# Two transformer blocks on one core: each stage's matmul operand is made around the border to it, and the router works on the raw residual

## The chip, the cores and the metric

One Trainium2 chip, of which the kernel uses one core. The time is that of the device for one launch, in microseconds (us); several runs are made and their median counts. A profile is one more execution, recorded by the hardware profiler. In its rows PE is TensorE's matmul stream, PEld its weight loads, DVE VectorE, ACT ScalarE, SPq the sequencer that issues the DMAs, L170 line 170 of the kernel.

## The reference, cut to what matters

256 tokens of width 1024 go through a first block (not touched here but for its last stages' form) and a second block of two layers, and everything is fp32. Layer one is an attention mix and a feed-forward; layer two is an attention with selected keys and a mixture of eight experts, two for each token. Each stage begins with a norm and a modulation by a vector `c`:

```
h = rms_norm(x, norm_mix) * (1 + sc_m) + sh_m
x = x + g_m * (attention(h @ w_in) @ w_out)
h = rms_norm(x, norm_ffn) * (1 + sc_f) + sh_f
x = x + g_f * swiglu(h, gate, up, down)          # layer one, 2816 wide
# layer two instead of it:
logits = h @ router_w + router_b
top_vals, top_idx = top_k(logits, 2); gates = softmax(top_vals)
x = x + g_f * sum_e combine[:, e] * swiglu(h, exp_gate[e], exp_up[e], exp_down[e])
```

## The kernel before, in words

The 256 tokens are two blocks of 128 (`tb` 0 and 1); the residual `h` stays in SBUF, tokens on the partitions. A product of fp32 numbers is made of three fp32r matmuls (`mm3`, L170 to L172): high part by high part, high part of the operand by low part of the weight, low by high. So each weight that a DMA brings in (`raw`) is split by ACT into a high part `wh` (L161) and by DVE into a low part `wl` (L162), and each operand likewise into `xh` and `xl`. There are 6 buffers for `wh`/`wl` and 6 pairs for operands.

`run(i)` calls the stages one after another: 0 to 4 are the first block, 5 its final norm (made together with the norm of stage 6), 6 `even_mix`, 7 `even_ffn`, 8 `odd_mix`, 9 `moe`, 10 the last norm. A border "6 to 7" is the place where stage 6's last product (`psacc`, four accumulators: two token blocks by two halves of 512 columns) is added to the residual and stage 7's first product starts. What lies between:

- `residual` or `gated_residual`: DVE adds each half to `h`.
- `follow`: the norm of the next stage, ACT's squares (L187), DVE's small `rsqrt` steps (L198 to L204), and `xn`, the normed rows (L264, or L279 in `normed_twice`). `normed_twice` writes the first norm times its gain into an extra tile and then rescales `h` with ACT (L280).
- `gate_rows` (L647, L648): the vector that gates the stage's result is spread over the partitions by two fp32 matmuls with a matrix of ones, and copied to SBUF by ACT.
- `to_T_mod`: eight PE transposes of `xn` per token block (L236), gain and shift on ACT and DVE (L253, L255), and the split into `xh` and `xl`. Then the first product starts for that block.

In `moe` the same is done with `xn`, but for the router (L1269): 8 transposes, modulations and 8 small fp32 matmuls with 8 columns per token block, then the two best scores (L1276 to L1279), the places of the tokens in each expert's list (`tri`, L1292), and the gather of each expert's tokens by matmuls with a 0/1 matrix `sel` (L1348, L1354). The program's text gives no fixed order: the tile framework's scheduler orders the instructions of each engine at build time, and every engine then works through its own row strictly in order. `issued_after(ins)` pins what is made inside it behind an instruction, `hold` pins the weight splits.

## Time and profile before

| | |
|---|---|
| median of 3 runs | 1831.12 us (1830.2 to 1831.45) |
| the profiled execution's own time | 1827.23 us |
| its span | 1825.3 us |
| PE busy | 1762.6 us, 97% |
| DVE busy | 1415.3 us, 78% |
| ACT busy | 1085.7 us, 59% |

The span is what the profile covers; the execution's own time is 1.9 us longer, and this execution was 3.9 us shorter than the median of the runs. [...]

### The profile page before, as it was taken

To read this page: it belongs to the slowest core of one execution; us is meant where nothing else is said; L and a number is where in the kernel's file an instruction comes from. 1 tells how busy PE (TensorE), PEld (TensorE's weight loads), DVE (VectorE), ACT (ScalarE), POOL (GpSimd) and SP (SyncE) were. 2 spreads that over 40 slices of the span, in tenths; PEclk is the share of its full clock that TensorE was granted. 3 is DMA by queue.
4 is the path that set the end of the run, shared out by engine and by line. 5 is a ranking of instruction groups with operands and counts; after the bars stand their busy time and mean duration, and the time that the engine had idled before them with its cause. 6 is when DMAs were issued, how large, how long until landed. Compare 5 with 4: busy or idle time off the path is not lost.

```text
span 1825.3 us, 24502 instructions
## 1 busy us (share of the span) xinstructions
PE 1762.6 (97%) x9045; PEld 1522.3 (83%) x9045; DVE 1415.3 (78%) x2505; ACT 1085.7 (59%) x1717; POOL 11.9 (1%) x37
## 2 busy tenths in 40 slices
PE   8999999999999999999989999999998999999996
PEld 6889788888889798888979878898887888888885
DVE  6658877678767797876777765547976999999997
ACT  5443654446445576554566754446485888877774
POOL 0000000000000000000010000000000000000000
PEclk9999999999999999999999999999998999999998
DMA  8768687667767415676755145555324999899993
GB/s 298 253 204 294 225 282 254 231 226 251 257 218 254 157 65 171 218 258 225 254 164 193 48 138 184 174 172 174 132 77 136 358 322 349 316 336 331 336 360 141
DMA packets 181030, 412.40 MB, mean 226 GB/s; under 512 B 8803, under 2 KB 59174, under 8 KB 180774
## 3 DMA queue, kind: packets, MB, share of 16 engines
q1 hardware_dynamic: 178694, 409.12, 64.7%
q10 hardware_dynamic: 2208, 1.63, 0.3%
q8 instruction: 73, 1.20, 0.3%
q14 instruction: 55, 0.45, 0.1%
HBM read 409.67 MB, written 1.05 MB: 225 GB/s over the span
## 4 chain that ended last, share of the span: by engine, by line
PE 83%; DVE 8%; ACT 5%; DMA 3%; issue 1%; SPq 0%; ACTq 0%; DVEq 0%
PE psa L170 17%; PE psa L171 17%; PE psa L172 17%; PE psacc L170 8%; PE psacc L171 8%; PE psacc L172 8%; PE pstr L236 3%; DVE wl L162 2%; ACT wh L161 2%; PE psa L1354 1%; DMA raw<-in_ffn_pre_wd 1%; DMA raw<-in_ffn_pre_wu 1%; ACT sg L789 1%; PE pstr L1385 1%; DVE big L588 1%
## 5 line engine op out<-in xcount | busy, mean ns | idle before, releaser
L162 DVE TENSOR_TENSOR wl<-raw,wh 128x1024 fp32r<-128x1024 f32 (+2 forms) x720 | 816.7, 1157 | 272.6 <-ACT wh L161 266.3
L161 ACT ACTIVATE wh<-raw 128x1024 fp32r<-128x1024 f32 (+2 forms) x720 | 712.1, 1008 | 502.9 <-PE psa L172 271.4
L170 PE MATMUL psa<-wh,xh 128*128 128x512 f32 (+3 forms) x1536 | 569.6, 372 | 16.6 <-ACT xh L161 11.0
L171 PE MATMUL psa<-wl,xh 128*128 128x512 f32 (+3 forms) x1536 | 564.3, 368 | 2.3 <-DVE wl L162 2.2
L172 PE MATMUL psa<-wh,xl 128*128 128x512 f32 (+3 forms) x1536 | 561.8, 368 | 0.0
L170 PEld LDWEIGHTS psa<-wh,xh 128*128 128x128 f32 x1536 | 290.4, 189 | 59.3 <-ACT xh L161 11.9
L171 PEld LDWEIGHTS psa<-wl,xh 128*128 128x128 f32 x1536 | 290.7, 189 | 41.5 <-DVE wl L162 5.4
L172 PEld LDWEIGHTS psa<-wh,xl 128*128 128x128 f32 x1536 | 290.0, 189 | 37.4 <-DVE xl L166 0.5
L170 PE MATMUL psacc<-wh,ah 128*128 128x512 f32 x616 | 239.2, 392 | 1.5 <-ACT wh L161 1.5
L171 PE MATMUL psacc<-wl,ah 128*128 128x512 f32 x616 | 240.3, 390 | 0.2
L172 PE MATMUL psacc<-wh,al 128*128 128x512 f32 x616 | 240.2, 390 | 0.0
L170 PEld LDWEIGHTS psacc<-wh,ah 128*128 128x128 f32 x616 | 115.4, 188 | 25.2 <-ACT wh L161 2.4
L171 PEld LDWEIGHTS psacc<-wl,ah 128*128 128x128 f32 x616 | 115.7, 188 | 24.4 <-DVE wl L162 1.1
L172 PEld LDWEIGHTS psacc<-wh,al 128*128 128x128 f32 x616 | 115.6, 188 | 24.3
L588 DVE SCALAR_TENSOR_TENSOR big<-raw,csil,big 128x1024 f32<-128x1024 f32 x84 | 107.6, 1281 | 2.7 <-DMA raw<-in_e_ada_w 1.3
L162 DVE TENSOR_TENSOR al<-pstr,ah 128x512 fp32r<-128x512 f32 (+2 forms) x92 | 54.1, 611 | 32.7 <-ACT ah L161 32.2
L236 PE MATMUL pstr<-ident,aa 128*128 128x128 f32 x432 | 64.3, 275 | 8.2 <-DVE aa L717 4.7
L236 PEld LDWEIGHTS pstr<-ident,aa 128*128 128x128 f32 x432 | 51.9, 141 | 16.7 <-DVE aa L717 3.0
L161 ACT ACTIVATE ah<-pstr 128x512 fp32r<-128x512 f32 (+2 forms) x92 | 46.2, 534 | 29.5 <-PE pstr L236 22.4
L171 PE MATMUL psacc<-wl,xh 128*128 128x512 f32 (+1 forms) x144 | 54.8, 380 | 0.0
L172 PE MATMUL psacc<-wh,xl 128*128 128x512 f32 (+1 forms) x144 | 54.6, 379 | 0.0
L170 PE MATMUL psacc<-wh,xh 128*128 128x512 f32 (+1 forms) x144 | 54.6, 385 | 0.0
(307 smaller groups left out, 1835.8 us busy)
## 6 DMA issues: line engine op xcount, KB each, us to landing
raw<-in_o_exp_down SPq DMA_DIRECT2D x40, 1024.0 KB, 6.4
raw<-in_o_exp_gate SPq DMA_DIRECT2D x32, 1024.0 KB, 6.7
raw<-in_o_exp_up SPq DMA_DIRECT2D x32, 1024.0 KB, 7.7
raw<-in_e_ada_w SPq DMA_DIRECT2D x24, 1024.0 KB, 7.2
raw<-in_o_ada_w SPq DMA_DIRECT2D x24, 1024.0 KB, 5.5
raw<-in_ffn_pre_wd SPq DMA_DIRECT2D x20, 1024.0 KB, 6.0
raw<-in_ffn_post_wd SPq DMA_DIRECT2D x20, 1024.0 KB, 4.9
raw<-in_ffn_pre_wu SPq DMA_DIRECT2D x16, 1024.0 KB, 5.3
```

The costliest lines, as they stand in the source:

```text
L161: nc.scalar.activation(H, src, AF.Copy)
L162: nc.vector.tensor_sub(L, src, H.bitcast(F32))
L170: mm(out, x[0], w[0], start=start, stop=False)
L171: mm(out, x[0], w[1], start=False, stop=False)
L172: mm(out, x[1], w[0], start=False, stop=stop)
L236: self.nc.tensor.transpose(out[:, j * P:(j + 1) * P], src[:, b * P:(b + 1) * P], self.ident)
L588: nc.vector.scalar_tensor_tensor(acc, src, self.csil[:, k:k + 1], acc, op0=ALU.mult, op1=ALU.add)
L789: nc.scalar.activation(sm[:, c], sm[:, c], AF.Exp, bias=ng[:, tb:tb + 1], scale=-1.0, accum_out=rs[:, tb:tb + 1])
L1354: nc.tensor.matmul(o[:, j * S:(j + 1) * S], XN[tb][part][:, (k + j) * P:(k + j + 1) * P], sel[tb], start=n == 0, stop=n == 3)
L1385: nc.tensor.matmul(t, selT[e][:, tb * P:(tb + 1) * P], y[hf][part], start=part == 0, stop=part == 1)
```

## The change

A class `Ahead` holds the norm and the operand of the next stage, and each is made once, by whoever asks first. The current stage's last product asks for the next stage's block 0 (`feed_next`) behind a named matmul of block 1, the next stage's product for block 1 behind the fifth of block 0's eight steps over `k` (three matmuls each). `gate_rows` now comes behind block 1's transposes. The last product runs its two halves in turn, so that the first 512 columns are done before the second begin, and each half's residual is added by itself, in PSUM and without a tile of its own. Its last two or three weight units use operand pairs instead of `wh`/`wl` buffers (`lent`). `normed_twice` works in `h` itself. In `moe` the router multiplies the transposes of the raw residual by weights into which gain and shift are folded (`router_load`, made during `odd_mix`), and the norm's factor `r` is applied to the eight scores.

```diff
+    class Ahead:
+        def __init__(self, net, norm, feed=None, raw=False):
+            self.net, self.calls, self.out, self.raw = net, (norm, feed), [{}, {}], raw
+        def do(self, i, tb):
+            if tb not in self.out[i]:
+                self.out[i][tb] = self.calls[i](tb) if i == 0 else self.calls[i](tb, self.norm(tb))
+            return self.out[i][tb]
...
+    def feed_next(self, ins):
+        if self.nxt and self.nxt.calls[1]:
+            with self.issued_after(ins):
+                self.nxt.feed(0)
...
     def normed_twice(self, tb):
-        t, x = self.xtile(tb), self.xtile(tb)
+        x = self.xtile(tb)
...
-            nc.vector.tensor_mul(t[:, c], h[:, c], self.gain[:, c])
+            nc.vector.tensor_mul(h[:, c], h[:, c], self.gain[:, c])
...
-        nc.scalar.activation(h, t, AF.Copy, scale=self.rsqrt(v1, D))
+        nc.scalar.activation(h, h, AF.Copy, scale=self.rsqrt(v1, D))
...
         for k, tb in self.order(KT, NT, feed):
-            if feed and k == 0:
-                feed(tb)
-            self.mm3(os[tb][:, :n], X.at(k, tb * P, P), ws[k], k == 0, k == KT - 1)
+            ins = self.mm3(os[tb][:, :n], X.at(k, tb * P, P), ws[k], k == 0, k == KT - 1)
+            if feed and tb == 0 and k == KT // 2:
+                with self.issued_after(ins):
+                    feed(1)
...
-    def gated_residual(self, tb, acc, g):
+    def gated_residual(self, tb, hf, acc, g):
...
-            t = self.fbuf("aa")
-            nc.vector.tensor_mul(t, acc[hf], g[:, c])
-            nc.vector.tensor_add(h[:, c], h[:, c], t)
-        self.follow(tb)
+        nc.vector.tensor_mul(acc, acc, g[:, c])
+        nc.vector.tensor_add(h[:, c], h[:, c], acc)
+        if hf == 1:
+            self.follow(tb)
...
+            for hf, j, tb in [(hf, j, tb) for hf in range(2) for j, tb in order] if last else \
+                    [(hf, j, tb) for j, tb in order for hf in range(2)]:
...
+                if last and tb == 1 and hf == 1 and j == 0:
+                    self.feed_next(ins)
...
+    def router_scores(self, tb, r):
...
+            self.transposes(t, h, range(4 * q, 4 * q + 4))
+            F = self.fbuf("aa")
+            if q:
+                nc.vector.tensor_copy(F, t)
+            else:
+                copied = nc.scalar.activation(F, t, AF.Copy)
...
+        nc.vector.scalar_tensor_tensor(l[:, :8], o[:, :8], r, rc, op0=ALU.mult, op1=ALU.add)
```

PE at the border 5 to 6, where `psacc` is the last product of stage 4, `xn` the normed rows and `psa` the first product of stage 6. Before:

```order
L172 MATMUL psacc_7470<-wh_8669,al_8750 128x512
L647 MATMUL pstr_8867<-sg_8866,hc 128x512
L647 MATMUL pstr_8875<-sg_8874,hc 128x512
L236 MATMUL pstr_8899<-ident,xn_8694 128x128 x4
L236 MATMUL pstr_8911<-ident,xn_8694 128x128 x4
L170 MATMUL psa_8897<-wh_8847,xh_8882 128x392
```

With the change, at the same place:

```order
L173 MATMUL psacc_7474<-wh_8663,al_8753 128x512
L276 MATMUL pstr_8789<-ident,xn_8697 128x128 x4
L276 MATMUL pstr_8801<-ident,xn_8697 128x128 x4
L171 MATMUL psacc_7474<-wh_8667,ah_8752 128x512
L172 MATMUL psacc_7474<-wl_8668,ah_8752 128x512
L173 MATMUL psacc_7474<-wh_8667,al_8753 128x512
L171 MATMUL psacc_7474<-wh_8673,ah_8752 128x512
L172 MATMUL psacc_7474<-wl_8674,ah_8752 128x512
L173 MATMUL psacc_7474<-wh_8673,al_8753 128x512
L171 MATMUL psa_8906<-wh_8877,xh_7016 128x392
```

The transposes of block 0 now stand ahead of the last six matmuls of the old stage, and the two gate matmuls are gone from the border. They stand 24 matmuls later, behind block 1's transposes:

```order
L173 MATMUL psa_8906<-wh_8891,xl_7019 128x392
L276 MATMUL pstr_8923<-ident,xn_8820 128x128 x4
L276 MATMUL pstr_8935<-ident,xn_8820 128x128 x4
L695 MATMUL pstr_8949<-sg_8948,hc 128x512
L695 MATMUL pstr_8957<-sg_8956,hc 128x512
L171 MATMUL psa_8907<-wh_8877,xh_7016 128x392
```

So all of block 0's 24 matmuls now lie ahead of block 1's transposes; before, block 1's first four transposes stood behind the second matmul of block 0. ACT's row at this border, with the change (`wh_8887` and `wh_8891` are weights of the new stage, `h_70` is block 0's residual, `aa` the modulated transposes):

```order
L188 ACTIVATE junk_8706,sm_8707<-h_70 128x512 x2
L162 ACTIVATE wh_8887<-raw_8885 128x784
L162 ACTIVATE wh_8891<-raw_8885 128x784
L188 ACTIVATE junk_8821,sm_8822<-h_71 128x512
L293 ACTIVATE aa_8794<-pstr_8789,mod_532,sm_8787 128x128
L293 ACTIVATE aa_8806<-pstr_8801,mod_532,sm_8787 128x128
L162 ACTIVATE wh_9027<-raw_9025 128x768
L320 ACTIVATE h_70<-h_70,sm_8744 128x1024
L293 ACTIVATE aa_8794<-pstr_8789,mod_532,sm_8787 128x128
L293 ACTIVATE aa_8806<-pstr_8801,mod_532,sm_8787 128x128
L162 ACTIVATE xh_7016<-aa_8794 128x4x128
```

Three weight splits and the rescaling of `h` stand between the squares and the operand `xh`. PE in the router, with the change (`psacc_13077` is block 1's second half of `odd_mix`, the L1335 rows are the scores):

```order
L173 MATMUL psacc_13077<-wh_13182,xl_12782 128x512
L276 MATMUL pstr_13347<-ident,h_71 128x128 x4
L1335 MATMUL psa_13342<-sm_12572,aa_13352 128x8 x4
L276 MATMUL pstr_13358<-ident,h_71 128x128 x4
L1335 MATMUL psa_13342<-sm_12572,aa_13363 128x8 x4
L1366 MATMUL pstr_13377<-sm_13372,hc 128x8
L1366 MATMUL pstr_13388<-sm_13372,hc 128x8
L695 MATMUL pstr_13397<-sg_13396,hc 128x512
L695 MATMUL pstr_13405<-sg_13404,hc 128x512
```

Block 0's transposes and scores stand ahead of this, among the last 15 matmuls of `odd_mix`; before, all transposes and scores of both blocks stood behind the last of them and behind the gates.

## Rows read from the trace of the kernel before

**Rows 1.** Busy time of each engine over the span.

```profile
PE 1762.6 (97%) x9045; PEld 1522.3 (83%) x9045; DVE 1415.3 (78%) x2505; ACT 1085.7 (59%) x1717; POOL 11.9 (1%) x37
```

**Rows 2.** Waits of PE: who for whom, total, times, longest.

```profile
PE psa L170 <- ACT xh L161: 11.0, 3, 5.7
```

**Rows 3.** Busy time by stretch: borders 5-6, 6-7, 7-8, 8-9, experts.

```profile
core 0: us, PE busy (x) PEld busy (x) DVE busy (x) ACT busy (x) POOL busy (x), PEclk, DMA share, GB/s
933.80:950.55 16.75, 10.97 (x45) 8.89 (x44) 12.89 (x49) 10.97 (x22) 0.00 (x0) 0.80 0.57 182
1058.90:1075.10 16.20, 12.10 (x46) 8.52 (x44) 12.57 (x30) 9.65 (x19) 0.00 (x0) 0.79 0.35 111
1249.00:1266.10 17.10, 14.04 (x72) 11.41 (x71) 15.60 (x39) 12.88 (x25) 1.14 (x4) 1.00 0.40 127
1380.20:1405.30 25.10, 19.32 (x96) 17.12 (x94) 17.82 (x62) 12.81 (x27) 0.00 (x0) 0.66 0.31 105
1405.30:1809.00 403.70, 400.56 (x1938) 341.27 (x1936) 375.07 (x409) 315.86 (x384) 0.00 (x0) 1.00 0.89 320
```

**Rows 4.** Timeline of border 5-6: start, duration, engine, line, tiles [idle before].

```profile
932.46 0.85 ACT L161 ACTIVATE wh<-raw 128x768 fp32r<-128x768 f32 x1 [0.38 <-PE psacc L172]
933.62 1.88 PE L647 MATMUL pstr<-sg,hc 128*128 128x512 f32 x4
...
934.68 0.74 DVE L279 TENSOR_SCALAR xn<-xn,sm 128x1024 f32<-128x1024 f32 x1
...
935.48 1.09 PE L236 MATMUL pstr<-ident,xn 128*128 128x128 f32 x8
...
936.19 0.63 ACT L187 ACTIVATE aa<-h 128x512 bf16<-128x512 f32 x1 [0.86 <-DVE h L346]
936.72 0.19 ACT L187 ACTIVATION_READ_ACCUMULATOR aa<-h 128x1 f32 x1
...
938.22 0.58 ACT L648 ACTIVATE big<-pstr 128x512 f32<-128x512 f32 x1
...
938.69 1.14 ACT L280 ACTIVATE h<-xn,sm 128x1024 f32<-128x1024 f32 x1
...
941.64 0.63 ACT L161 ACTIVATE xh<-aa 128x512 fp32r<-128x512 f32 x1
...
942.17 0.44 ACT L253 ACTIVATE aa<-pstr,mod,sm 128x128 f32<-128x128 f32 x1
...
942.32 0.69 PE L170 MATMUL psa<-wh,xh 128*128 128x392 f32 x1 [5.75 <-ACT xh L161]
```

**Rows 5.** PE's timeline at border 6-7.

```profile
1062.54 1.06 PE L236 MATMUL pstr<-ident,xn 128*128 128x128 f32 x8 [1.74 <-DVE xn L264]
1065.88 0.80 PE L170 MATMUL psa<-wh,xh 128*128 128x512 f32 x1 [2.28 <-ACT xh L161]
```

**Rows 6.** PE's timeline at border 7-8.

```profile
1256.71 1.04 PE L236 MATMUL pstr<-ident,xn 128*128 128x128 f32 x8
1260.73 0.44 PE L170 MATMUL psa<-wh,xh 128*128 128x384 f32 x1 [2.98 <-ACT xh L161]
```

**Rows 7.** Timeline of PE and DVE in the router.

```profile
1380.88 0.68 DVE L356 TENSOR_TENSOR aa<-psacc,big 128x512 f32<-128x512 f32 x1
...
1383.77 0.63 PE L236 MATMUL pstr<-ident,xn 128*128 128x128 f32 x4 [1.73 <-DVE xn L264]
...
1387.07 3.29 PE L1269 MATMUL psa<-sm,aa 128*128 128x8 f32 x14
...
1405.27 0.48 PE L170 MATMUL psa<-wh,xh 128*128 128x512 f32 x1
```

**Rows 8.** PE's timeline at the border from the pool mixer to the feed-forward.

```profile
223.54 0.50 PE L170 MATMUL psa<-wh,xh 128*128 128x512 f32 x1 [0.79 <-ACT xh L164]
```

**Rows 9.** Timeline of a late expert's last product, PE and DVE.

```profile
1662.28 3.49 DVE L162 TENSOR_TENSOR wl<-raw,wh 128x1024 fp32r<-128x1024 f32 x3
...
1663.55 0.50 PE L171 MATMUL psacc<-wl,ah 128*128 128x512 f32 x1
```

## What the change should do to the time

> **What bounds the kernel now.** I read the busy times first. PE is busy 97% of the span [rows 1], so a change can only pay where PE stands still or runs at half clock, and about 60 us of idle PE is all that there is. The experts' phase holds none of it worth taking: 400.56 of 403.7 us busy at full clock [rows 3]. Then I asked what PE waits for. The largest entry is the first product's wait for `xh`: 11.0 us in three waits, the longest 5.7 [rows 2]. The timeline shows all three at the second block's borders: 5.75 at border 5-6 [rows 4], 2.28 at 6-7 [rows 5], 2.98 at 7-8 [rows 6]. Last I asked for the stretches around the borders [rows 3], and there the clock is the second thing to see. Over the border 5-6 the mean granted clock is 0.80, over 6-7 0.79, over the router 0.66, and over 7-8 1.00. [...]
>
> So each border now loses this. 5-6: 16.75 less 10.97 busy is 5.8 idle; of the 6.7 us at half clock about 6 are busy and cost half of that, 2.9: together **8.7 us**. 6-7: 16.2 less 12.10 is 4.1 idle; of 6.8 us at half clock some 5.5 are busy and cost 2.75: **6.85**. 7-8: 2.98 idle at full clock: **3.0**. Router: 25.1 us from the last product to the first expert's matmul.
>
> **Border 5-6: a loss of 2.0.** The transposes of block 0 move into the old product, the gates behind block 1's transposes, and neither is what PE waited for: it waited for ACT. With the change, ACT's row between the squares and `xh` holds two weight splits of 128x784, a square of block 1, two modulations, a third split, the rescaling of `h`, two modulations and the split itself. By the durations of [rows 4]: 2 x 0.85 + 0.82 (0.63 and 0.19) + 0.88 + 0.85 + 1.14 + 0.88 + 0.63 = 6.9 us. They start when the first weight unit of the last product is let go, which is six matmuls and eight transposes ahead of its end: 6 x 0.21 (matmuls overlap; the experts' 1938 take 400.56 us [rows 3]) + 1.09 = 2.4 us. So PE waits 4.5 us for block 0. Then 24 matmuls run, and DVE's row has an instruction that reads their sum ahead of block 1's `xn`; behind it stand four steps of `rsqrt` of about 0.2 and `xn` at 0.74 [rows 4], so block 1's transposes wait 1.5 us. Behind them come the gates, 1.88 on PE, and ACT's row has gate copy 0.58 (which waits for half of the gates, 0.95), modulations 0.88, rescaling 1.14, modulations 0.88 and split 0.63: 5.1 us, of which the gates cover 1.9, so 3.2 us of waiting. Sum 9.2 at full clock, against 8.7 now: +0.5. If the clock falls as long as it does now, 2.9 more: +3.4. The longest wait gets shorter (4.5 against 5.75), yet there are three of them; I take the middle, **+2.0**.
>
> A row bears on this: at 6-7 PE idled 1.74, did eight transposes in 1.06, idled 2.28, and ran at half clock afterwards, though no idle time by itself was as long as the 2.98 at 7-8 which had no such consequence [rows 3, 5, 6]. [...]
>
> **Border 6-7: 0.** Block 0's `xn` stands in DVE's row between two residual halves of block 1 and comes about 0.95 us after the last product; the eight transposes follow (1.06), and ACT then needs a modulation, a square, two modulations and the split, 0.46 + 0.82 + 0.92 + 0.63 = 2.8, 3.0 with handing over. Block 1's transposes and the gates now stand behind 15 matmuls, and the nine that remain cover its operand but for 0.3. Idle: 4.25 against 4.1. No matmul runs for 0.95 + 1.06 + 3.0 = 5.0 us, and none for 1.74 + 1.06 + 2.28 = 5.1 now, so I let the clock fall as before. Bounds: -2.6 if it stays full, +0.2.
>
> **Border 7-8: +0.6.** Block 0's transposes move into the old product, and the operand (two squares, two modulations, the split: 0.63 + 0.19 + 0.92 + 0.63, 2.6 with handing over) is what PE then waits for; the second half of the operand, its low part and block 1 add 0.35 + 0.25 + 0.35 by my estimate from the same durations. Sum 3.55 against 2.98. The clock held there and I let it hold; if it falls, 6.8 us at half speed cost up to 3.4 more.
>
> **Router: -6.5.** This is where the change has a dependence to remove: the scores no longer wait for `xn`, only for `h`. Block 0's transposes and scores (2.8 us of PE work) now lie inside `odd_mix`'s last product. After its end remain, in one chain: gated residual of the last half, 2 x 0.68 [rows 7]; transposes 0.63; copy to SBUF 0.6; eight score records, 8 x 3.29/14 = 1.9 at half clock [rows 7] and 0.95 at full; the second transposes and copy hide behind the first scores but for about 0.9, then 0.95 of scores again; scale, two best, compare: seven small DVE steps of 0.1 to 0.2, 1.2 us; the places by two small matmuls 0.5 and one DVE step 0.2; `sel` 0.3; the gather, 32 matmuls of 256 columns at half the 0.21, 3.4, and four transposes, 0.63. The two gate matmuls run while PE waits for `sel`. Sum 11.6, and some 2.2 for some ten handings over between engines: 13.8 us. Against 25.1 less the 2.8 moved: **-8.5**. If the clock falls here too, PE's own 6 us in this stretch grow by 3.0: -5.5. Every stretch of the same make ran at half clock (0.66 in the router now [rows 3]), but with more idle time: I take -6.5.
>
> **The rest.** The 0.79 wait from the pool mixer to the feed-forward [rows 8] is filled with six matmuls of the old stage: -0.8. `router_load` puts some ten small DVE operations into `odd_mix`: +0.3 (0 to 0.7). Pinning at the start: +0.1. Experts: their weight use moves by one or two matmuls at most where weights are late, because the scheduler weaves the halves there again; the splits hide behind PE. +0.2 (0 to 3). The other feed-forward borders keep their order to within a matmul: 0; so does the tail.
>
> **Sum.** 2.0 + 0 + 0.6 - 6.5 - 0.8 + 0.3 + 0.1 + 0.2 = **-4.1 us**. Against the profiled execution's own 1827.23 that is 1823.1; that execution lay 3.9 under the median of the runs, which the new time will be compared with, so 1831.12 - 4.1 = **1827.0**. What a measurement can tell from no change is about 0.2%, 3.7 us.
>
> **The rivals.**
>
> *The clock stays full.* If the waits, cut into pieces, no longer bring half clock at 5-6, 6-7 and the router: +0.5 - 2.6 + 0.6 - 8.5 - 0.8 + 0.4 = -10.4, so 1820.7. For it: 2.98 us of waiting at 7-8 left the clock at 1.00 [rows 3, 6]. Against it: 1.74 and 2.28 with only transposes between did not [rows 5].
>
> *Waits swapped for waits.* What ACT does at the borders stays the same, only at other places; 5-6 at +3.4, 7-8 with a fall of the clock at +4.0, the router at -5.5: with the rest -0.2, about +1.7, so 1832.8, no change that could be measured. For it: ACT and DVE are busy two thirds to three quarters of these stretches [rows 3]; PE is not what they wait for.
>
> *The halves in turn starve the experts.* In the last product of an expert the first 512 columns now want the second and third weight unit earlier, by three and six matmuls of 0.21: 0.6 and 1.3 us. For it: in a late expert the second unit's `wl` is made from 1662.28 on, three splits in 3.49, so the first ends at about 1663.45, and PE takes it at 1663.55 [rows 9]: nothing to spare. DVE is 93% busy in this phase [rows 3]. Fully paid, 8 x 1.3 = 10.4 us: 1837. It decides the sign from 4.1 / 8 = 0.5 us an expert on, and makes the kernel measurably slower from (4.1 + 3.7) / 8 = 1.0 on. Against it: with the change, PE's row at this place has both halves woven, the second unit's low part at the ninth matmul as before; only in early experts, where the splits are further ahead, do they run in turn.
>
> **How the numbers follow.** The forecast, the border terms above within their bounds, 1823.5 to 1830: 0.46, and 0.26 of it beyond 0.2% faster, 0.20 within. The clock stays full, 1819 to 1823.5: 0.19, all faster. Waits swapped, 1830 to 1834.8: 0.23, within. Experts starved, above 1834.8: 0.12. So faster 0.45, no change 0.43, slower 0.12. Leaving out the last and the lower part of the second, the range is **1820 to 1834**.
>
> **What would show each step.** In the changed profile PE's wait at 5-6 should come in three pieces, about 4.5, 1.5 and 3.2, the first and last released by ACT's `xh`. At 6-7 one of about 1 before the transposes and one of 3 behind them. The router's stretch, from the end of `odd_mix`'s last product to the first expert matmul, should measure 14 to 17 us; the granted clock in it tells which. Over the experts PE should still be over 99% busy. I am wrong if ACT's row at the borders gets its operand out earlier than these sums say, since then two to five us more are gained at each border; or if waits of PE for `wl` (L172) appear among the experts.

## The result and the profile after

The changed kernel took 1841.84 us (median of 4 runs, 1840.29 to 1844.25) against 1830.66 us of the kernel before on the same chip: ratio 1.0067, 95% interval 1.0053 to 1.0082. It is slower by about 12 us, where 4 us faster was forecast and 1834 was the top of the range. One execution of the kernel before, beside the experiments e5 to e8 below, took 9972.77 us and is left out of their ratios.

The page of the changed kernel, its first part (answers to [rows 1]), and PE's waits, longest in total first (answers to [rows 2]):

```profile
PE 1771.4 (96%) x9047; PEld 1522.6 (83%) x9047; DVE 1418.2 (77%) x2503; ACT 1080.8 (59%) x1707; POOL 12.4 (1%) x37
```

```profile
PE psa L171 <- ACT xh L162: 11.5, 5, 3.5
PE psa L173 <- DVE xl L167: 7.2, 13, 0.9
PE psa L171 <- ACT xh L165: 4.4, 5, 1.7
PE psa L172 <- DVE wl L163: 4.2, 7, 1.3
PE pstr L575 <- DMA aa<-in_ffn_pre_norm: 3.9, 1, 3.9
PE pstr L1315 <- DVE sm L1313: 3.5, 1, 3.5
```

The first of these is the one that the prediction worked on: 11.0 us in three waits before, 11.5 in five now, none as long as the longest before. The second was 0.2 us in one wait before, and the sixth is new. `xl` of line 167 is the low part of an operand of the first block, which the prediction passed over, and line 1315 is the small matmul of `router_load`.

The same stretches as in [rows 3], now with the changed kernel's times (borders 5-6, 6-7, 7-8, router, experts):

```profile
954.90:973.30 18.40, 10.82 (x44) 8.31 (x43) 14.32 (x50) 11.59 (x26) 0.00 (x0) 0.91 0.19 58
1079.80:1096.20 16.40, 12.77 (x52) 9.16 (x51) 12.84 (x34) 9.78 (x21) 0.00 (x0) 0.90 0.19 64
1272.00:1289.60 17.60, 15.26 (x79) 12.50 (x79) 14.05 (x30) 12.34 (x27) 0.00 (x0) 1.00 0.37 118
1405.50:1421.70 16.20, 12.68 (x74) 9.40 (x73) 11.91 (x38) 7.92 (x14) 0.00 (x0) 0.89 0.06 7
1421.70:1826.00 404.30, 400.98 (x1936) 341.34 (x1936) 376.28 (x420) 315.23 (x384) 0.00 (x0) 1.00 0.90 322
```

PEclk, the number ahead of the last two, is the granted TensorE clock as a share of full speed. In the traces of these two kernels it is 1.00 or 0.50 at any time (0.50 from 961.00 to 964.40 at border 5-6 of the changed kernel), and a value between is the mean of a stretch that held both. The stretches do not all begin and end at the same matmuls as in [rows 3], so their lengths alone are no comparison. The router's, which does, fell from 25.1 to 16.2 us, and its clock rose from 0.66 to 0.89. The borders 5-6 and 6-7 have a higher clock too. The second block got faster, as forecast, as the next table shows, and border 5-6 begins at 954.9 where it began at 933.8: the loss is all in the first block.

To see where, I matched the same matmul (the one of `xh` with `wl` in each group of three; there are 2656 of them in both traces) and took the difference of its start. The two traces exaggerate the loss: the changed kernel's profiled execution took 1844.25, 2.4 us more than its median, and that of before 3.4 less than its. At 219.5 us, ahead of most of the differences between the kernels, the offsets of all the traces of this study lie between -0.9 and +4.8, so a single offset says little; the steps from place to place say more. At 932.5 the transposes of block 0 (1.03 us), which the change moves into the old product, are already behind the changed kernel: at 930 its offset is +21.5.

| place in the program | start before | change | e1 | e6 |
|---|---|---|---|---|
| end of the pool mixer | 219.5 | +1.8 | +0.9 | -0.4 |
| start of the first block's second layer | 415.0 | +5.4 | +1.4 | +1.2 |
| end of that feed-forward | 604.3 | +12.0 | +2.3 | +1.9 |
| in the attention | 657.4 | +15.9 | +4.5 | +2.1 |
| last product of the first block | 932.5 | +22.4 | +5.4 | +2.9 |
| end of `even_mix` | 1057.8 | +22.2 | +6.7 | +4.1 |
| end of `even_ffn` | 1249.8 | +20.9 | +6.2 | +3.6 |
| in `odd_mix`, behind the query products | 1351.1 | +23.0 | +8.4 | +2.7 |
| end of `odd_mix` | 1379.7 | +25.9 | +11.3 | +5.5 |
| first expert | 1405.6 | +16.4 | +1.8 | -3.9 |
| last expert | 1808.2 | +16.9 | +2.0 | -3.7 |

The loss comes in four jumps, each within some 25 us: +3.2 and +6.5 and +5.3 at the starts of the feed-forward stages at 220, 415 and 740 us, and +3.9 at the attention's first projection behind 604. (e1 and e6 are experiments, below.) The largest, at 418 us of the changed kernel, in PE's timeline:

```profile
418.31 1.03 PE L276 MATMUL pstr<-ident,h 128*128 128x128 f32 x8
420.07 0.50 PE L171 MATMUL psa<-wh,xh 128*128 128x512 f32 x1 [0.72 <-ACT xh L165]
420.41 0.40 PE L172 MATMUL psa<-wl,xh 128*128 128x512 f32 x1
421.51 0.49 PE L173 MATMUL psa<-wh,xl 128*128 128x512 f32 x1 [0.71 <-DVE xl L167]
422.14 0.50 PE L171 MATMUL psa<-wh,xh 128*128 128x512 f32 x1
422.48 0.40 PE L172 MATMUL psa<-wl,xh 128*128 128x512 f32 x1
423.40 0.51 PE L173 MATMUL psa<-wh,xl 128*128 128x512 f32 x1 [0.53 <-DVE xl L167]
423.81 0.50 PE L171 MATMUL psa<-wh,xh 128*128 128x512 f32 x1
424.14 0.40 PE L172 MATMUL psa<-wl,xh 128*128 128x512 f32 x1
425.24 0.80 PE L173 MATMUL psa<-wh,xl 128*128 128x512 f32 x1 [0.70 <-DVE xl L167]
425.83 0.63 PE L171 MATMUL psa<-wh,xh 128*128 128x512 f32 x1
...
428.95 1.91 PE L276 MATMUL pstr<-ident,h 128*128 128x128 f32 x8
```

Each of the first three steps of three matmuls stops at its third, which needs the low part `xl`; the fourth waits 0.19 there and the fifth not at all. DVE's timeline at the same place shows why it is late: pairs of low parts stand 1.85 us apart, with a weight split or a modulation step between.

```profile
421.11 0.60 DVE L167 SCALAR_TENSOR_TENSOR xl<-pstr,cols,xh 128x128 fp32r<-128x128 f32 x2
421.63 0.20 DVE L190 TENSOR_SCALAR sm<-sm 128x1 f32<-128x1 f32 x1
421.86 1.23 DVE L163 TENSOR_TENSOR wl<-raw,wh 128x1024 fp32r<-128x1024 f32 x1
423.00 0.60 DVE L167 SCALAR_TENSOR_TENSOR xl<-pstr,cols,xh 128x128 fp32r<-128x128 f32 x2
...
423.65 1.27 DVE L636 SCALAR_TENSOR_TENSOR big<-raw,csil,big 128x1024 f32<-128x1024 f32 x1
424.84 0.60 DVE L167 SCALAR_TENSOR_TENSOR xl<-pstr,cols,xh 128x128 fp32r<-128x128 f32 x2
```

In the kernel before, at the same start, block 1's transposes stand behind the second and third matmul of block 0, and each third matmul comes without a wait:

```profile
414.64 0.50 PE L170 MATMUL psa<-wh,xh 128*128 128x512 f32 x1 [0.53 <-ACT xh L164]
414.98 0.39 PE L171 MATMUL psa<-wl,xh 128*128 128x512 f32 x1
415.21 0.71 PE L236 MATMUL pstr<-ident,h 128*128 128x128 f32 x5
415.67 0.48 PE L172 MATMUL psa<-wh,xl 128*128 128x512 f32 x1
415.99 0.49 PE L236 MATMUL pstr<-ident,h 128*128 128x128 f32 x3
```

With the change, after five steps the pinned transposes of block 1 come, 428.95, and by then PE runs at half clock (0.50 from 425.11 to 431.94): the matmuls of 0.40 have become 0.63, and start 0.43 apart instead of 0.23. Over this stretch, PE was busy 17.01 of 20 us at a clock of 0.83. The kernel before, in the stretch that begins equally far ahead of its first matmul, was busy 19.47 of 20 at full clock:

```profile
416.80:436.80 20.00, 17.01 (x64) 12.17 (x63) 13.74 (x33) 11.27 (x26) 0.00 (x0) 0.83 0.52 173
```

```profile
411.50:431.50 20.00, 19.47 (x93) 15.86 (x92) 18.70 (x40) 14.37 (x30) 0.00 (x0) 1.00 0.74 249
```

The cause stands in the diff at a place that the front quotes only for `lin`: `swiglu`, which the first block's feed-forward uses too, got the same pin, and the first block's attention projection goes through `lin`.

### The profile page after: what moved, and what is told of

It is laid out like the page before. It is cut to its first block, busy times and chain, and to the rows that moved or that the text cites. A ratio compares the mean times of both kernels' runs of the same rounds, so it can differ in the third digit from the quotient of the medians.

```text
span 1842.4 us, 24491 instructions
## 1 busy us (share of the span) xinstructions
PE 1771.4 (96%) x9047; PEld 1522.6 (83%) x9047; DVE 1418.2 (77%) x2503; ACT 1080.8 (59%) x1707; POOL 12.4 (1%) x37
## 4 chain that ended last, share of the span: by engine, by line
PE 83%; DVE 9%; ACT 4%; DMA 3%; issue 1%; SPq 0%; ACTq 0%; DVEq 0%
PE psa L173 17%; PE psa L172 17%; PE psa L171 17%; PE psacc L172 8%; PE psacc L173 8%; PE psacc L171 8%; PE pstr L276 3%; DVE wl L163 2%; ACT wh L162 1%; DVE big L636 1%; DMA raw<-in_ffn_pre_wd 1%; PE psa L1429 1%; DVE xl L167 1%; ACT sg L834 1%; PE pstr L1460 1%
## 5 line engine op out<-in xcount | busy, mean ns | idle before, releaser
L163 DVE TENSOR_TENSOR wl<-raw,wh 128x1024 fp32r<-128x1024 f32 (+2 forms) x705 | 798.7, 1156 | 276.6 <-ACT wh L162 271.2
L162 ACT ACTIVATE wh<-raw 128x1024 fp32r<-128x1024 f32 (+2 forms) x705 | 695.6, 1007 | 493.7 <-PE psa L173 258.9
L171 PE MATMUL psa<-wh,xh 128*128 128x512 f32 (+2 forms) x1536 | 572.9, 373 | 16.9 <-ACT xh L162 11.5
L172 PE MATMUL psa<-wl,xh 128*128 128x512 f32 (+2 forms) x1536 | 566.9, 369 | 4.3 <-DVE wl L163 4.2
L172 PE MATMUL psacc<-wl,ah 128*128 128x512 f32 x572 | 222.9, 390 | 0.2
L173 PE MATMUL psacc<-wh,al 128*128 128x512 f32 x572 | 222.9, 390 | 0.0
L171 PE MATMUL psacc<-wh,ah 128*128 128x512 f32 x572 | 222.2, 391 | 0.0
L172 PEld LDWEIGHTS psacc<-wl,ah 128*128 128x128 f32 x572 | 107.4, 188 | 22.9 <-DVE wl L163 1.1
L173 PEld LDWEIGHTS psacc<-wh,al 128*128 128x128 f32 x572 | 107.4, 188 | 22.4
L188 ACT ACTIVATE junk<-h 128x512 bf16<-128x512 f32 x48 | 30.1, 628 | 40.8 <-DVE h L388 17.6
```

The source lines that it names most:

```text
L162: nc.scalar.activation(H, src, AF.Copy)
L163: nc.vector.tensor_sub(L, src, H.bitcast(F32))
L171: mm(out, x[0], w[0], start=start, stop=False)
L172: mm(out, x[0], w[1], start=False, stop=False)
L173: return mm(out, x[1], w[0], start=False, stop=stop)
L188: nc.scalar.activation(junk[:, :m], x[:, c], AF.Square, scale=scale, accum_out=ss[:, i:i + 1])
```

## The experiments

Theory A: the pin. In the kernel before, block 1's transposes run behind the second and third matmul of block 0, and PE then weaves the matmuls of both blocks, six for each step, so the low parts may come at DVE's pace. With the pin PE has three matmuls for each step and nothing else until the fifth. Theory B: the halves in turn and the lent buffers make the next stage's weights late. Theory C: DVE's work for the modulation vectors, between the low parts, is the cause.

| run | median us | ratio to before | 95% interval |
|---|---|---|---|
| e1 change, feed-forward of block one unpinned | 1830.58 | 1.0000 | 0.9991 to 1.0010 |
| e2 before, with that pin alone | 1840.14 | 1.0053 | 1.0036 to 1.0070 |
| e3 change, whole last down in block one | 1836.35 | 1.0038 | 1.0018 to 1.0057 |
| e4 e1, `router_load` late | 1827.65 | 0.9986 | 0.9975 to 0.9997 |
| e5 e1, attention projection unpinned | 1828.36 | 1.0001 | 0.9990 to 1.0011 |
| e6 e4 and e5 together | 1824.66 | 0.9978 | 0.9966 to 0.9990 |
| e7 e6, rescaling of `h` late | 1822.89 | 0.9973 | 0.9961 to 0.9985 |
| e8 e6, old router | 1832.08 | 1.0024 | 1.0013 to 1.0036 |
| e9 before, pin behind step 2 | 1835.84 | 1.0027 | 1.0014 to 1.0040 |
| e10 before, pin behind step 8 | 1847.57 | 1.0101 | 1.0086 to 1.0117 |
| e11 e7, no pin in block two either | 1827.29 | 0.9988 | 0.9979 to 0.9998 |
| e12 change, modulation work behind | 1838.49 | 1.0052 | 1.0038 to 1.0066 |

Kernels were run in groups of one to four beside the kernel before, whose medians in these groups were 1830.03 (e1 to e4), 1828.96 (e5 to e8), 1829.65 (e9 to e11) and 1829.13 (e12); across groups the ratios are compared.

**e1: the first block's feed-forward without the pin.**

```diff
-                if feed and i == k == tb == 0 and not up:
-                    feed(0)
+                if feed and i == k == 0 and not up and (tb == 0 or r is not None):
+                    feed(tb)
...
-                if feed and i == tb == 0 and k == KT // 2 and not up:
+                if feed and i == tb == 0 and k == KT // 2 and not up and r is None:
```

> The changed kernel, but the first block's four feed-forward stages ask for block 1's transposes where the kernel before does, ahead of block 1's first matmul and not pinned behind the fifth step of block 0; all else as changed. Theory A (the pin takes away the matmuls of block 1 that filled PE's waits for block 0's operand): about 19 of the 22 us that the first block lost come back, so 1821 to 1825, and PE's waits of the first product for xl (13 of them, 7.2 us) fall to three or fewer. Theory B (the last down's halves in turn and the lent buffers bring the next stage's weights and residual late): no more than 3 us back, 1839 to 1842. Theory C (the small DVE work for the modulation vectors, which stands between the operand's splits, is what holds PE): the waits stay, since that work stays, 1838 or more.

1.0067 became 1.0000: 0.67%, 12 us, came back with this one edit; 19 had been expected, worked out from the 22 us of two traces that exaggerate by 5.8. The waits for `xl` at this line fell from 13 with 7.2 us to 3 with 1.4. PE's timeline of e1 at the same start:

```profile
416.01 0.50 PE L171 MATMUL psa<-wh,xh 128*128 128x512 f32 x1 [0.72 <-ACT xh L165]
416.35 0.39 PE L172 MATMUL psa<-wl,xh 128*128 128x512 f32 x1
416.58 1.03 PE L276 MATMUL pstr<-ident,h 128*128 128x128 f32 x8
417.46 0.50 PE L173 MATMUL psa<-wh,xl 128*128 128x512 f32 x1
418.09 0.50 PE L171 MATMUL psa<-wh,xh 128*128 128x512 f32 x1
418.43 0.40 PE L172 MATMUL psa<-wl,xh 128*128 128x512 f32 x1
418.66 0.44 PE L171 MATMUL psa<-wh,xh 128*128 128x512 f32 x1
418.94 0.39 PE L172 MATMUL psa<-wl,xh 128*128 128x512 f32 x1
419.17 0.39 PE L171 MATMUL psa<-wh,xh 128*128 128x512 f32 x1
```

The transposes fill the first wait, and then there are always two kinds of matmul ready that need no low part. DVE in this run gives ten low parts in a row in 2.70 us. C as it was put (the work stays, so the wait stays) falls, and B with it.

**e2: the pin alone, in the kernel before.**

```diff
-                if feed and i == k == 0 and not up:
+                if feed and i == k == 0 and not up and (tb == 0 or r is None):
                     feed(tb)
...
+                if feed and i == tb == 0 and k == KT // 2 and not up and r is not None:
+                    with self.issued_after(ins):
+                        feed(1)
```

> The kernel before with one edit: in the first block's feed-forward stages block 1's transposes are pinned behind the fifth step of block 0. Theory A: 16 to 20 us slower than before, 1847 to 1851, lost at the starts of the stages at about 223, 415, 615 and 745 us. Theory B: within 2 us of before, since halves and buffers are untouched. Theory C: within 4 us of before.

10 us slower, 1.0053: the direction and the place are A's, the size is 60% of what A said. The jumps in its trace at the three feed-forward starts are +3.8, +3.1 and +3.8 (the attention's projection, which has no pin here, shows none), and PE's clock over the 20 us from 411.5 stayed at 1.00. e3 looks into what the changed kernel loses beyond these.

**e3: the pin kept, the last down product as before.**

```diff
-                    lambda tb: None if start and tb == 0 else feed(tb), 2)
+                    lambda tb: None if start and tb == 0 else feed(tb))
...
-            for hf, j, tb in [... for j, tb in order] if last else \
+            for hf, j, tb in [... for j, tb in order] if last and job[2] is None else \
```

> The changed kernel without halves in turn and without lent buffers in the first block's last down products; the pin stays. Theory A: the loss at the four stage starts stays, 1839 to 1844. Theory B: 15 us or more come back, below 1828.

1.0038 against the change's 1.0067 (the intervals just overlap): most of the loss stays, so B is not the cause, but about 5 us of it goes, which A alone had not said; 1836 lies in neither theory's range. At the start near 415 us PE is busy 17.97 of 20 us in e3, at full clock, where the change had 17.01 at 0.83:

```profile
414.50:434.50 20.00, 17.97 (x80) 12.96 (x80) 17.94 (x38) 13.50 (x29) 0.00 (x0) 1.00 0.78 266
```

At the start near 755 us the clock fell in e3 too, to 0.93 over 23 us (0.85 in the change), behind waits for `xl` of 0.87 and 0.65 that the change has as 0.86 and 0.65. So a longer time at half clock is part of what these two executions of the change and e3 differ by; that the halves in turn bring it is not shown. Without the pin the halves cost little at the starts: in e1, which has them, the offset changes by +0.2, +0.3 and -0.4 over the three.

**e4: the router's folded weights made later.** On top of e1:

```diff
-        self.router_load()
         heads = []
...
-            heads.append(((lambda: turn_queries(1)) if hd == 3 else None, ...
+            heads.append(({3: lambda: turn_queries(1), 8: self.router_load}.get(hd), ...
```

> The kernel of e1 and one more edit: the router's folded weights are made at the ninth head of the selected-key attention instead of ahead of the first. In the changed profile a small matmul of this folding stands at the head of the attention in PE's row and waits 3.5 us for DVE; in the kernel before, PE waits 1.7 us there for other things. If the matmul's place is the cause: 1.5 to 3 us faster than e1. If DVE, which is full in this stretch, is the cause: within 0.7 us of e1, and another row waits as long at the same place.

2.9 us faster than e1 by the medians (0.9986 against 1.0000, the intervals touching). In the changed kernel this row is the longest wait in `odd_mix`, with the first matmuls of the attention's scores queued behind it (the one small matmul is recorded as two):

```profile
1344.13 0.56 PE L1315 MATMUL pstr<-sm,hc 128*128 128x8 f32 x2 [3.54 <-DVE sm L1313]
1344.54 0.56 PE L171 MATMUL psa<-xh,xh 128*128 128x256 f32 x1
```

In e4 it is gone, and PE's largest wait in the 6 us from its place on is 1.45 us, for the transposes of the next queries. Over the same stretch, 1300 to 1351 us, the offset grows by 2.7 in the change and 2.9 in e1 and falls by 0.3 in e4 and e6. The place was the cause, as expected; e4 moves the folding's DVE operations together with its matmul, so it does not tell the two apart.

**e5 and e6: the attention projection unpinned, without and with e4's edit.**

```diff
...
+            if feed and not pin and tb == 1 and k == 0:
+                feed(1)
...
-            if feed and tb == 0 and k == KT // 2:
+            if feed and pin and tb == 0 and k == KT // 2:
...
```

> The kernel of e1, and the first block's attention projection gets block 1's transposes ahead of block 1's first matmul as in the kernel before, since the same pin sits in that product's loop too. In e1's trace the stage around 605 to 640 us is still 3 us longer than before, and block 1's transposes stand there behind the pinned matmul. If the pin is the cause there as well: 2 to 4 us faster than e1, 1826.5 to 1828.5, and the offset against the kernel before after this place falls from about 4.5 to under 2.5 us. If it is the halves in turn or the per-half residual: within 1 us of e1.

> All pins of the first block undone, and the router's folded weights made at the ninth head (e4 and e5 together). If the two repairs are independent the sum of their gains holds: 1830.6 - 2.9 - 3 = 1824.7, 1823 to 1826.5, faster than the kernel before by 0.2 to 0.4%. If they share a wait: about 1827.

By the ratio e5 is no faster than e1, where 2 to 4 us had been expected. In the traces the stretch from 604 to 633 us, which is 3.0 us longer in e1 than before, is 0.4 shorter in e5 and 0.2 longer in e6, and over all the traces the five with this pin (the change, e1, e3, e4, e12) gain 2.6 to 3.9 us of offset there, the eight without it -0.6 to +0.2. So the step itself is there; but e5's profiled execution had lost 2.1 us more than e1's by 220 us, ahead of any difference between the two programs, and scatter of this size may hide it in the time. e6 against e4 is 0.9978 to 0.9986. The 3 us are seen in the traces and are not settled in the time. e6 as a whole comes out where expected, 4 us faster than before.

**e7: the rescaling of `h` behind the split.**

```diff
-        nc.scalar.activation(h, h, AF.Copy, scale=self.rsqrt(v1, D))
+        r1 = self.rsqrt(v1, D)
+        self.resc[tb] = lambda: nc.scalar.activation(h, h, AF.Copy, scale=r1)
...
+                if tb in self.resc:
+                    with self.issued_after(self.last_split):
+                        self.resc.pop(tb)()
```

> The kernel of e6, with the rescaling of h at the border 5 to 6 pinned behind the operand's split on ACT. If the rescaling (1.14 us) is what block 1's operand waits for, PE's last wait there (2.78 us in the changed kernel) falls by about 1.1 and the first (3.49) by 0.3, since a weight split takes the freed place: 1 to 2 us faster than e6. If DVE's row sets it: within 0.5 us of e6.

1.8 us by the medians, inside what was expected, though the intervals of e6 and e7 overlap. PE's three waits at border 5-6 are these, changed kernel first (e6 has the same three values):

```profile
959.68 0.44 PE L171 MATMUL psa<-wh,xh 128*128 128x392 f32 x1 [3.49 <-ACT xh L162]
967.36 1.06 PE L276 MATMUL pstr<-ident,xn 128*128 128x128 f32 x8 [1.21 <-DVE sm L204]
972.92 0.45 PE L171 MATMUL psa<-wh,xh 128*128 128x392 f32 x1 [2.78 <-ACT xh L162]
```

```profile
939.85 0.44 PE L172 MATMUL psa<-wh,xh 128*128 128x392 f32 x1 [3.19 <-ACT xh L163]
948.27 1.06 PE L280 MATMUL pstr<-ident,xn 128*128 128x128 f32 x8 [2.11 <-DVE sm L205]
952.10 0.45 PE L172 MATMUL psa<-wh,xh 128*128 128x392 f32 x1 [1.04 <-ACT xh L163]
```

The first wait fell by 0.30 and the last by 1.74, where 0.3 and 1.1 had been expected, and the middle one rose by 0.90, which had not: together 1.1 us less. Over the border the offset falls by 0.5 where e6's grows by 2.2; the waits are 1.1 of that, and how much of the rest is the edit's is not shown, since the clock over the 24 us from 935.5 was higher too (0.93 against 0.86). e7 is the fastest kernel of the study, 0.27% under the kernel before.

**e8: the old router in e6.** The scores are made of the normed rows again, with the code of before; the experts are as changed.

> The kernel of e6 with the old router: transposes of the normed rows, modulation, scores behind the last product, gates ahead of them. By the traces the stretch from the last product to the first expert shrank by 9.4 us and 2.9 us of it moved into the product, a net of 6.5. If the raw residual is what gains it: 5.5 to 8 us slower than e6, 1830 to 1833. If the gates' new place or the halves in turn gain most: less than 3 us slower.

7.4 us slower than e6 (1.0024 against 0.9978, intervals apart). In the traces, from 1351.1 to the first expert, the offset falls by 1.6 in e8 and by 6.6 in e6, and among the experts it grows by 1.7 against 0.3. So the new router pays, and the halves in turn, which e8 keeps, are not what pays. The raw residual alone is not shown: e8 puts the gates back ahead of the transposes too, where they take PE 1.88 us with the transposes following at once, so up to 1.9 of the 7.4 may be the gates' place.

**e9 and e10: the pin of e2 behind another step.** `k == 1` and `k == KT - 1` instead of `k == KT // 2`.

> The kernel before with the first block's feed-forward pin behind the second step of block 0 (six matmuls) in place of the fifth (15; that one was 10 us slower than before in e2). If PE loses because it has no matmul of block 1 while block 0's operand comes step by step, the loss grows with the number of steps ahead of the pin: here 1 to 5 us slower than before. If any pin costs the same: 9 to 11.

> The same with the pin behind block 0's last step (24 matmuls). By the theory of the missing matmuls: 14 to 20 us slower than before, since all eight steps then run at the operand's pace and block 1's operand is exposed behind them. If the cost comes from the place of the transposes alone: 9 to 11, as in e2.

6, 10 and 18 us by the medians for a pin behind step 2, 5 and 8 (0.27%, 0.53%, 1.01%; the intervals of e2 and e10 are apart, those of e9 and e2 overlap a little). The loss grows with the number of steps without block 1, as A says; a pin that costs the same at any step would have given 9 to 11 each time. The first steps cost more than the 1 to 5 expected.

**e11: no pin in the second block.** In e7 the conditions of both pins set to never.

> The kernel of e7 with the second block's pins undone too: block 1's transposes are asked for ahead of block 1's first matmul at all three borders. In PE's row they then stand at the same place at border 5 to 6, nine matmuls later at 6 to 7 and five later at 7 to 8, so block 1's operand is less covered there: 1 to 4 us slower than e7. If the pin costs in the second block what it cost in the first: faster than e7 by 1 us or more.

0.9988 against 0.9973: slower by about 2.7 us by the ratios, with intervals that overlap a little. What is wrong in the first block is right, or at least no harm, in the second, where block 1's transposes would otherwise stand still later in PE's row. In the traces 1.3 us of it lie at border 6-7; at 7-8 and the router, where most of the rest lies, the clock was lower in e11 as well (0.94 and 0.80, against 1.00 and 0.89 in e7).

**e12: all pins kept, the modulation work held back.**

```diff
+            self.last_L = nc.vector.scalar_tensor_tensor(L, src, scale, H.bitcast(F32), op0=ALU.mult, op1=ALU.subtract)
...
+                with self.issued_after(self.last_L):
+                    if k == 0:
+                        nc.vector.tensor_scalar(acc, src, self.csil[:, 0:1], None, op0=ALU.mult)
...
```

> The changed kernel with every pin kept, but DVE's work for the modulation vectors (1.28 us each) pinned behind the last low part of the operand made ahead of it, so that it no longer stands between block 0's low parts. In the changed profile these parts come 1.85 us apart: 0.6 for a pair of them and 1.25 for other work between. If PE lost because block 1's matmuls were missing and the pace hardly matters: within 3 us of the changed kernel, 1.0055 to 1.0085 of before. If DVE's other work between the parts is the whole cause, with the pin only letting it in: 7 us or more back, 1.000 to 1.003 of before. In between, both are needed, and the waits of PE for xl fall by about half, since a weight split stands between the first two pairs as well.

1.0052 against 1.0067: 3 us by the ratios, and the intervals overlap. In DVE's timeline of e12 the third and fourth pair follow 0.8 us apart, and at the start near 418 us PE waits for `xl` once, 0.71 us, in place of four times. Total waits for `xl` at this line fall from 7.2 to 4.5. The clock falls at this start all the same, to 0.91 over the 20 us from 414. So both have a part: DVE's pace makes the wait, and block 1's matmuls are what used to hide it. With the pin kept and DVE's other work held back, about 9.5 of the 12 us stay; with the pin gone (e1) none do.

## Why the prediction was wrong

**The step that failed** is the sentence "The other feed-forward borders keep their order to within a matmul: 0". Their order does not hold. In the kernel before, block 1's transposes at this start stand behind two and three matmuls of block 0; with the change they stand behind fifteen (420.07 to 428.95 in the timeline above). What came in place of the 0: waits of PE for `xl` of 7.2 us where there had been 0.2, and stretches at half clock at two of the starts (0.50 for 6.83 us from 425.11 and from 763.03, means of 0.83 over 20 us and 0.85 over 23).

I read the order at the second block's borders, because that is where the waits of [rows 2] were, and took the first block's for given. A wait that is not in the trace of before is no sign that nothing holds it off: there it was held off by block 1's matmuls, and the edit took those away. Its price is 12 us in the change (e1), 10 alone (e2), and some 3 more in the traces at the attention's projection (e5 and e6), which the times do not settle.

**The second miss** is `router_load`, +0.3 in the sum and 2.9 by e4. I counted its DVE operations as work and not its one matmul as a place in PE's row, with all of the scores behind it.

**The third miss** is the -0.8 at the pool mixer [rows 8]. The wait of 0.79 was to be filled with six matmuls of the old stage. They came behind the first two matmuls of the new one, and the wait is 0.52 in the change and in e6. Over 219.5 to 245 us the offset changes by 0 to +0.3 in the kernels without the feed-forward's pin (e1, e4 to e8, e11).

**What held.** From 930, ahead of border 5-6, to 1808.2 the trace gives -4.6 us (+21.5 to +16.9), `router_load`'s loss included; the terms of the second block added up to -3.4. But the trace of before, from which the prices were read, was itself a lucky execution here. From 930 us on, PE's row in e2, e9 and e10 is that of the kernel before, the same 4417 records in the same order, and PE's wait at border 7-8 is the same (2.96 to 2.98). Yet over that stretch the clock was 0.91 in all three, where it had been 1.00 [rows 3]; in e9:

```profile
1254.50:1273.20 18.70, 15.65 (x73) 13.02 (x71) 15.64 (x39) 12.92 (x25) 1.17 (x4) 0.91 0.44 136
```

Over the router it was 0.61, for 0.66 in the kernel before, and from 930 to 1808.2 the offsets of the three grow by 3.3, 5.1 and 4.5. So "the clock held there" told of one execution, and against such traces the second block's gain would be 3 to 5 us larger than by this one.

- Border 5-6, forecast +2.0: from 930 to 1000 us of the kernel before, so with the transposes that moved, the offset changes by +0.8 in the change and by +2.2 in e1 and e6, with the same three waits in all of them; over 24 us from the last product on the clock was 0.93 in the change and 0.86 in e1 and e6. The three waits came as forecast, 3.49, 1.21 and 2.78 for 4.5, 1.5 and 3.2, released by ACT, DVE and ACT. The clock was 0.91 over 18.4 us, with 0.50 from 961.00 on for 3.4 us, where the kernel before had it for 6.83. The first wait was oversized by 1.0.
- Border 6-7, forecast 0: waits of 0.90 and 2.69, for 0.95 and 3.0; the offset falls by 1.3 in the change and by 0.5 in e1 and e6. The clock fell as assumed, but for half as long: 0.50 from 1087.30 on for 3.4 us, where the kernel before had it for 6.83 (0.90 over 16.4 us). It fell 1.35 us into the first product (1085.95), behind the two waits with the eight transposes (1.06 us from 1082.20 on) between them. It also fell behind the 3.49 at border 5-6, which has six matmuls between it and the transposes. I let it fall at 6-7 because no matmul of a product runs there for 5.0 us; that this decides it was my assumption, and these traces do not show it.
- Border 7-8, forecast +0.6: the wait was 2.23, for 2.6, the 0.95 that was to come on top did not show, and the offset falls by 0.6, the other way.
- Router, forecast -6.5: 25.9 to 16.4 is -9.4 over the stretch, and 2.9 of it had moved into `odd_mix`'s last product (+23.0 to +25.9): -6.5. The stretch measured 16.2 us, within the 14 to 17 forecast. e8 gives 7.4 by the medians for the new router as a whole.
- Experts, forecast +0.2: +0.5. The rival of the starved experts did not come; PE is busy 400.98 of 404.3 us. Its sign, waits for `wl` among the experts, did show: 2.7 us in five waits, where the kernel before has 1.2 in five.
- The rival of the full clock came in part: 0.91, 0.90 and 0.89 at 5-6, 6-7 and the router, where it had been 0.80, 0.79 and 0.66.

With the first two misses mended, e6 is 4.0 us faster than before by its ratio, where the sum had said 4.1. That these agree so well is in part luck: in e6's trace the first block is still 2.0 us behind at 930, where the sum had it 0.7 ahead, and the second block gains 5.7 where it had 3.4. Of the rivals none named the first block; the range ended at 1834 because every bound in it was of the second.

The times at half clock in the prediction's losses of now, 6.7 us at border 5-6 and 6.8 at 6-7, are worked out from the means in [rows 3]. The trace of before shows 0.50 over 6.83 us at each, from 941.80 and from 1064.65, with PE busy for 6.28 and 5.52 of them, where about 6 and 5.5 had been taken.

Four readings in the working are loose, and none decides the result. ACT and DVE were not busy two thirds to three quarters of the stretches but half (ACT, router) to nine tenths (DVE, 7-8) by [rows 3]. Not every stretch of the same make ran at half clock: 0.66 is a mean that held 17.07 us at 0.50 (from 1385.50), and 7-8 was at 1.00. The sum of the full-clock rival, -10.4, leaves out the experts' +0.2. And the 0.2 us for a handing over between engines (ten of them, 2.2 us, in the router) was my estimate from no row: in the changed kernel's router PE starts 0.05 and 0.06 us behind the copies that ACT and DVE end at 1407.26 and 1410.14.

## What to carry to other kernels

A pin in a helper acts on every caller: look at the order at each of them, also where the trace shows no wait, and ask of every row that moves what it was filling. An operand that is made step by step can need a second stream of matmuls beside it, as it did in this first block and not in the second (e11); its steps came every 1.85 us here, one block's three matmuls, 0.23 apart, filled 0.7 of them and two blocks' six 1.4. And a tiny instruction is costed by its place in an in-order row, not by its duration: the 0.56 us matmul of `router_load` held PE for 3.5.

## What was not expected of the hardware

The clock fell with no long wait. Ahead of the half-clock stretch, which begins at 425.11 us, the longest idle time of PE was 0.72 us, and three others were 0.53 to 0.71 (the last of them, 0.70, ends at 425.24), with matmuls between all of them. In the windows of the changed kernel, PE was busy 3.14 of the 5.9 us ahead of it, and then at 0.50:

```profile
419.30:425.20 5.90, 3.14 (x9) 1.27 (x8) 5.87 (x14) 3.67 (x10) 0.00 (x0) 0.99 0.71 202
425.20:432.00 6.80, 6.57 (x19) 4.96 (x20) 3.87 (x13) 1.94 (x7) 0.00 (x0) 0.50 0.82 289
```

In e2, e3 and e10 the 5.9 us that begin equally far ahead of the first matmul were busy 4.48, 4.40 and 4.47, and the clock stayed at 1.00; at border 7-8 one wait of 2.23 us left it at 1.00 in the change, and one of 2.98 in the kernel before [rows 6].

But what PE did just ahead does not settle it in these traces. The 2.98 of the kernel before, repeated in e9 with the same row, had the clock fall. And in e12 PE did the same up to 421.15 as in the change up to 422.14: the eight transposes, an idle time of 0.72, two matmuls, one of 0.71, a third. There the clock fell in e12 (0.51 from 421.15 to 424.30), and in the change only 3 us later:

```profile
420.53 0.49 PE L174 MATMUL psa<-wh,xl 128*128 128x512 f32 x1 [0.71 <-DVE xl L168]
421.15 0.77 PE L172 MATMUL psa<-wh,xh 128*128 128x512 f32 x1
```

So the same work may keep the full clock in one execution and not in another, and what decides it is not shown by these runs.
